# Mixer 0 of a hybrid decoder step: steps of joins, sample and group norms placed between the hops of a chunked scan

## The chip, the cores and the metric

The kernel runs on one core of a Trainium2 chip. The metric is device time in microseconds (us) of one execution; the median of three runs before the change is 1593.11 us (1591.4 to 1595.03). Engines are named as the profile names them: PE is TensorE's matrix multiplication and PEld its weight load, DVE is VectorE, ACT ScalarE, POOL GpSimd, and SP the engine that issues most of the DMAs.

## The reference

One inference step of a two-layer recurrent decoder for 512 prompt tokens and 8 samples of 4 tokens. Layer 0 mixes with two head groups beside each other: Hawk's RG-LRU (A) and RWKV-7 (B), with one input projection and one output projection. Layer 1 is HGRN2; each layer is followed by a SwiGLU feed-forward network. Everything is float32. Cut to the mixer that the change touches:

```python
def _rwkv_step(S, inp):
    r_t, w_t, k_t, v_t, kk_t, a_t = inp
    sk = jnp.einsum('bhvk,bhk->bhv', S, kk_t)
    S = (S * w_t[:, :, None, :] - sk[..., None] * (kk_t * a_t)[:, :, None, :]
         + v_t[..., None] * k_t[:, :, None, :])
    return S, jnp.einsum('bhvk,bhk->bhv', S, r_t)
...
for l in range(DEPTH):
    xn = rmsnorm(x, P['ln_mix'][l])
    if l % 2 == 0:
        p = xn @ P['w_in_ab'][j]
        u, conv_new = causal_conv(p[..., :W_A], conv_st[j], P['conv_w'][j], P['conv_b'][j])
        h, h_new = rg_lru(u, h_st[j], ...)
        out_a = jax.nn.gelu(p[..., W_A:P_A]) * h
        out_b, rS_new, shift_new = rwkv7(p[..., P_A:], shift_st[j], rS_st[j], ...)
        y = jnp.concatenate([out_a, out_b], axis=-1) @ P['w_out_ab'][j]
    ...
    x = x + y
    xf = rmsnorm(x, P['ln_ffn'][l])
    x = x + (silu(xf @ P['ffn_gate'][l]) * (xf @ P['ffn_up'][l])) @ P['ffn_down'][l]
```

In `rwkv7` the heads' output goes through a group norm per head, then a bonus term and a gate.

## The kernel before

Layer 0's mixer runs from the start to about 410 us, and only it is touched. A dense product is one 128x128 weight tile against 272 columns; float32 precision is kept by splitting weights into a high and a low half (`wh`, made by ACT at L210, and `wl = wf - wh`, made by DVE or POOL at L213), so each tile takes three products, wh twice and wl once.

RWKV-7 runs in chunks. For the 512 prompt tokens there are 8 chunks of 64. `scan()` (L881) works through them; each chunk c has three hops on PE with copies on DVE between them:

- hop A: S·W (last state S) is added to V·KB (the values V) in one half, `cr`, of a PSUM bank, and DVE copies it to `rhs` (L907); V·TM goes to the other half, `cs`;
- hop B: T·rhs, and DVE copies the result to `U` (L917);
- hop C: U·TM is added to `cs`, and DVE adds the decayed old state to it, the new `S` (L923); then V·KB of the next chunk and twelve groups of output products `ops`.

Between the hops `self.fill(18)` takes 18 dense products out of a list of other work: `rglru` (L1068), the input columns of group A, its convolution (`cf`, `uc`), gates (`gate`), recurrence (`v`, L1127) and GELU, and after it `lead` (L1148), the first blocks of the output projection (`acc<-cat`).

Beside the scan there are three more pieces, Python generators that advance by one step per `next`:

- `join(g)` (L771), four steps for each half of the chunks, which put together the triangular inverse `T` out of 32x32 blocks (`jps`);
- `sample()` (L986), the 8 samples: products `rpss`, `sps`, `opss`, a group norm, and for each pair of heads p an expansion `vx` on POOL, a product `dpss` on PE, an addition into the state `S0` on DVE (L1064) and its store `rS_s` on SP (L1065);
- `groupnorm(o)` (L942), whose first part (`g` in the plan) takes statistics in small operations on DVE and normalises `o` on POOL (L966), and whose second part (`h`) transposes on PE (`tps`), multiplies by the gate's weights (`gps`) and finishes on ACT and DVE (L979 to L984).

Two strings set the order. `MID` orders the features ahead of the scan ("a", "b", "r", "R" are steps of a head pair's features, "j" a join step, "x" values, "g" the output gate). `PLAN` orders the rest: "c" a chunk, "j" a join step, "s" a sample step, "f" a fill, "g" and "h" the parts of a group norm, "l" the start of `lead`, "d" the drain of the list. From "r3" in `MID` to the end of `PLAN`, `self.in_order` is "all": each PE instruction is chained to the one before it, so PE keeps the order of the code. After that only dense products are chained, and a scheduler places the rest. DVE, ACT, POOL and SP follow the scheduler throughout, each in one fixed order once built.

`lead` opens a pool `wo` for the weights of its second and third output column. That pool takes the room that `sample()` closes at its end.

Of the kernel before, what the change touches and what calls it, by code (L numbers as in the profile page):

```python
# [15 lines left out]
OP = mybir.AluOpType  # L16
# [7 lines left out]
NB = 8  # L24
NS = 4
NT = SEQ + NB * NS
# [7 lines left out]
NCH = SEQ // CH  # L34
# [16 lines left out]
AHEAD = 1  # L51
SQP = 6
VTB = 2
MID = 'v0 v2 v3 a3 v1 A3 b3 a1 r3 B3 A1 b1 a2 r0 R3 B1 A2 x b2 a0 x r1 x B2 A0 b0 R0 j x j r2 x j R1 j B0 g R2'
ENG = dict(d=1, kh=1, w0=1, w1=0, sg=1, tw=0, kf=2, km=1, kb=0, al0=1, al1=0, g1=0, g2=1, g3=0, oa=1, sp0=1, sp1=1)
LO = (3, 1)
FEAT = 'f0 b0 f2 f1 b1 b2 n0 f3 b3 n1'
PLAN = 'c1 j1 f12 j1 f8 c1 j1 f4 j1 s1 c1 s1 g0 c1 s3 h0 c1 s4 g1 c1 h1 s4 c1 s3 g2 l3 c1 c1 h2 f20 d0'
MSB = 3
HOP = (18, 18, 18)  # L60
KHB = 2
# [75 lines left out]
class Build:  # L137
# [205 lines left out]
    def mixer0(self):  # L343
# [4 lines left out]
        PTT = nc.gpsimd.tensor_tensor  # L348
# [390 lines left out]
        def receptance(p):  # L739
            rm = ph.tile([128, NT], F32, tag="pr", name="rm", bufs=RMB)  # L740
            proj(p, rm)
            E(f"w{p % 2}")(W[p][:, :, CH:], chunks(rm), chunks(eb[p][:, 1:]), OP.mult)
            for par in range(2):
                r = par_rows[par]
                PTT(Ws[par][p][r, CB:], rm[r, SEQ:], eb[p][r, 1 + SEQ:], OP.mult)
            pr = rm
            STT(pr, rm, v("rk", p), bon[p], op0=OP.mult, op1=OP.mult)
            yield
            scores(p)
            for h in range(2):  # L750
                c = slice(h * HF, (h + 1) * HF)
                ps = mps("bops")
                self.mm(ps[:, :HF], block64, pr[:, c])
                TT(bon[p][:, c], ps[:, :HF], vm[p][:, c], OP.mult)
# [129 lines left out]
        def first():  # L884
            return tc.high_priority(offset=CHAIN_PRIO)

        def scan():
            ops = S = None
            Vs = {}

            def inputs(c):
                heads(cr, lambda p: KB[p][:, 0, c], Vs[c], True, c == 0)

            with first():
                for c in range(nv - 1):
                    Vs[c] = load_v(c)
            yield
            for c in range(NCH):
                V = Vs[c]
                rhs = z.tile([128, 4, 64], F32, tag="rhs", name="rhs", bufs=2)  # L900
                U = z.tile([128, 4, 64], F32, tag="U", name="U", bufs=2)
                with first():
                    if c == 0:
                        inputs(0)
                    else:
                        heads(cr, lambda p: W[p][:, c, 0:CH], S, False, True)
                    nc.vector.tensor_copy(rhs, cr)  # L907
                    heads(cs, lambda p: TM[p][:, 0, c], V, True, False)
                    if c:
                        sp = z.tile([128, 4, 64], F32, tag="sp", name="sp")  # L910
                        PTT(sp, S, ebT[:, :, c:c + 1].to_broadcast([128, 4, 64]), OP.mult)
                self.fill(HOP[0])
                with first():
                    for p in range(4):
                        for r in par_rows:
                            self.mm(cr[r, p], T[r, c, p], rhs[r, p], start=False, stop=True, chain=True)
                    nc.vector.tensor_copy(U, cr)  # L917
                self.fill(HOP[1])
                with first():
                    heads(cs, lambda p: TM[p][:, 1, c], U, False, True)  # L920
                    Sn = z.tile([128, 4, 64], F32, tag="S", name="S", bufs=2)
                    if c:
                        TT(Sn, cs, sp, OP.add)  # L923
                    else:
                        nc.vector.tensor_copy(Sn, cs)
                    if c % 2 == 0:
                        ops = op.tile([128, 2, 4, 64], F32, tag="o", name="ops")
                    if c + 1 < NCH:
                        inputs(c + 1)
                    outputs(c, V, S, U, ops)  # L930
                    if c + nv - 1 < NCH:
                        Vs[c + nv - 1] = load_v(c + nv - 1)
                S = Sn
                if c % 2:
                    o = kp.tile([128, 8, 64], F32, tag="o", name="o", bufs=2)
                    ACT(o, ops.rearrange("p c q v -> p (c q) v"), AF.Copy)
                    obuf[c // 2] = o
                if c == NCH - 1:
                    nc.sync.dma_start(self.o["rS_p"], S)
                self.fill(HOP[2])  # L940
                yield
# [44 lines left out]
        def sample():  # L986
# [61 lines left out]
                ACT(o[:32, par::2], ops[q_rows[par]], AF.Copy)  # L1048
            yield
            yield from groupnorm(o, 32, 4)  # L1050
            for p in range(4):
                yield
                vx = sm.tile([128, NB, 64], F32, tag="vx", name="vx")
                for par in range(2):
                    sr = sc_rows[par]
                    PTT(vx[sr], zc[par][sr, p][:, None, :].to_broadcast([64, NB, 64]),
                        seqsel[sr][:, :, None].to_broadcast([64, NB, 64]), OP.mult)
                dp = self.ms.tile([128, NB, 64], F32, tag="m", name="dpss")
                for par in range(2):
                    sr = sc_rows[par]  # L1060
                    self.mm(dp[par_rows[par]], TMs[p][sr], vx[sr])
                sf = S0[:, p]
                PTT(sf, sf, ebT[:, p, NCH:][:, :, None].to_broadcast([128, NB, 64]), OP.mult)
                TT(sf, sf, dp, OP.add)  # L1064
                nc.sync.dma_start(self.o["rS_s"][:, p], sf)  # L1065
            self.close("sample")

        def rglru(i, before):  # L1068
# [100 lines left out]
        for e in PLAN.split():  # L1169
# [18 lines left out]
                next(halves[n])  # L1188
            else:
                next(halves[n], None)  # L1190
        self.in_order = self.last = None
        nc.sync.dma_start(self.o["shift_o"], shift_sb)
        nc.sync.dma_start(self.o["conv_o"], conv_sb)
        nc.sync.dma_start(self.o["h_o"], h_sb)
# [1 line left out]
        self.ms = self.open("ms", bufs=4, space=PSUM)  # L1196
        self.op = self.open("ops", space=PSUM)
        self.late_pools()
        for _ in groupnorm(obuf[3], 128, 3):
            pass  # L1200
        self.dump("oa0", oa[0], (128, NT))
        self.dump("ob0", bon[0], (128, NT))
        self.dump("ob3", bon[3], (128, NT))
        self.hilo(cat[7], oa[3])
        for j in range(4):
            self.hilo(cat[3 + j], bon[j], H1)
        self.lo_pool = 0
        return cat, ww0, ps0

    def late_pools(self):  # L1210
        self.np_ = self.open("norm")
# [9 lines left out]
        self.hilo_scaled(a, x, self.v(g, k))  # L1221
        return a

    def out_proj0(self, cat, ww, banks):
        nc = self.nc
        W = self.i["w_out_ab"]
        self.x = []
        xg = []
        self.norm_begin(self.sqp)
        H0, H1 = slice(0, SPLIT), slice(SPLIT, NT)  # L1230
        n = len(ww)
        pool = (self.open("wo2"), (2, 2 * (LEAD - n)))
        ww += [self.column(W[m], 0, KT, pool) for m in range(n, LEAD)]
        for m in range(KT):
            x = self.xp.tile([128, NT], F32, name=f"x{m}")
            nc.sync.dma_start(x, self.i["xT"][:, m, :])
            self.x.append(x)

        def run(m, ps, ks, c, first, last):
            for _ in self.products(ps, ww[m], cat, ks, c, first, last):  # L1240
                pass
            if last:
                x = self.x[m][:, c]
                nc.vector.tensor_tensor(x, ps[:, :c.stop - c.start], x, OP.add)

        def bank(i):
            if i % 7 < 3:
                return self.acc.tile([128, 512], F32, tag="acc", name="acc", bufs=3)
            return self.ms.tile([128, 512], F32, tag="m", name="acc")
        self.in_order = "chain"  # L1250
        for m in range(n):
            run(m, banks[m], (7,), H0, False, True)
        for m in range(n, LEAD):
            run(m, bank(m), range(KT), H0, True, True)
        banks = [bank(m + LEAD) for m in range(LEAD)]
        for m in range(LEAD):
            run(m, banks[m], (0, 1, 2, 7), H1, True, False)
        for m in range(LEAD):
            run(m, banks[m], (3, 4, 5, 6), H1, False, True)
            xg.append(self.finish_x(self.x[m], m, "ln_ffn0", self.act_b))  # L1260
        self.in_order = self.last = None
        self.wide = True
        for m in range(LEAD, KT):
            def ev(ps, h, c):
                nc.vector.tensor_tensor(self.x[m][:, c], ps, self.x[m][:, c], OP.add)
            self.dense(W[m], cat, ev)
            xg.append(self.finish_x(self.x[m], m, "ln_ffn0", self.act_b))
        self.close("wo2", "wo", "keep")
        return xg
# [501 lines left out]
```

## Time and profile before

| what | value |
| --- | --- |
| median of 3 runs | 1593.11 us |
| the profiled execution | 1591.88 us |
| its span in the trace | 1590.1 us |
| around the span | 1.8 us |
| PE busy | 1495.7 us, 94% |
| DVE, ACT, POOL busy | 832.9, 547.7, 402.0 us |
| HBM read and written | 120.13 and 10.50 MB, 82 GB/s |
| mean granted clock of PE | 0.963 of full |

The profile is of one execution. Its page gives the busy time of each engine, then the span in 40 slices of about 40 us, where a digit is the busy share in tenths and `PEclk` the clock that PE was granted, in tenths of full speed. A list of instructions gives start and duration in microseconds, engine, line, operation, result and operands (numbers of buffers left out), shape, and in brackets the idle time before it with what ended that. "x16" is a run of sixteen. In the trace a small float32 product counts twice as many PE instructions as in the program.

### The profile page before, as it was taken

How to read it: one execution, taken by the hardware profiler on the slowest of the kernel's cores; microseconds unless marked ns; L12 is line 12 of the kernel's file. 1: busy time of each engine (PE TensorE's matmuls, PEld its weight loads, DVE VectorE, ACT ScalarE, POOL GpSimd, SP SyncE). 2: the span in 40 equal slices, each digit the busy share in tenths (PEclk: the TensorE clock that was granted, in tenths of full speed). 3: DMA queues.
4: the chain of work that ended last, by engine and by line, in shares of the span. 5: the costliest groups of instructions: out<-in, count | busy, mean ns of one | idle time of the engine just before them, and what ended most of it. 6: DMA issues, size and time to landing. Idle time of an engine off the chain costs nothing.

```text
span 1590.1 us, 34915 instructions
## 1 busy us (share of the span) xinstructions
PE 1495.7 (94%) x14688; PEld 1441.9 (91%) x14688; DVE 832.9 (52%) x1542; ACT 547.7 (34%) x982; POOL 402.0 (25%) x520
## 2 busy tenths in 40 slices
PE   7988888675999999999999999999999999999998
PEld 6877777555999999999999999999999999999997
DVE  7775344355454434443467657666675443444344
ACT  5642144134333223322344333333443322233234
POOL 4572243331211001100123344444441110110010
PEclk9997999777999999999999999999999999999999
DMA  4122221013022322322223222222333223222321
GB/s 161 61 69 83 57 77 35 24 58 104 30 91 85 90 88 85 94 87 87 91 82 113 69 98 92 79 89 95 103 118 97 85 87 91 90 93 82 93 74 57
DMA packets 87405, 132.88 MB, mean 84 GB/s; under 512 B 24369, under 2 KB 30385, under 8 KB 87121
## 3 DMA queue, kind: packets, MB, share of 16 engines
q1 hardware_dynamic: 87248, 130.66, 26.4%
q8 instruction: 115, 1.88, 0.5%
q14 instruction: 42, 0.34, 0.1%
HBM read 120.13 MB, written 10.50 MB: 82 GB/s over the span
## 4 chain that ended last, share of the span: by engine, by line
PE 78%; DVE 2%; ACT 1%; DMA 1%; POOL 1%; issue 0%; DVEq 0%; POOLq 0%; ACTq 0%; SPq 0%
PE acc L179 70%; PE lv L179 2%; PE ops L179 1%; PE ch L179 1%; DMA wf<-w_out_ab 1%; PE dpss L179 0%; PE ds L179 0%; PE tr L1586 0%; PE gps L179 0%; PE nps L179 0%; PE opsm L179 0%; PE d L179 0%; PE opsq L179 0%; DMA x<-xT 0%; PE gate L179 0%
## 5 line engine op out<-in xcount | busy, mean ns | idle before, releaser
L179 PE MATMUL acc<-xg,wh 128*128 128x272 f32 x4544 | 884.1, 293 | 11.6 <-ACT xg L270 6.4
L179 PEld LDWEIGHTS acc<-xg,wh 128*128 128x128 f32 x4544 | 721.3, 191 | 20.4 <-ACT xg L270 6.4
L179 PE MATMUL acc<-xg,wl 128*128 128x272 f32 x2272 | 652.1, 292 | 0.0
L210 ACT ACTIVATE wh<-wf 128x512 fp32r<-128x512 f32 (+1 forms) x404 | 250.8, 621 | 683.7 <-PE acc L179 546.1
L179 PEld LDWEIGHTS acc<-xg,wl 128*128 128x128 f32 x2272 | 429.8, 191 | 3.1 <-issue 0.8
L213 DVE TENSOR_TENSOR wl<-wf,wh 128x512 fp32r<-128x512 f32 (+1 forms) x373 | 267.5, 718 | 194.8 <-ACT wh L210 169.6
L1290 POOL TENSOR_TENSOR S<-S,rstd 128x272 f32<-128x272 f32 x88 | 74.6, 848 | 645.2 <-ACT S L1289 645.2
L179 PE MATMUL acc<-h,wh 128*128 128x272 f32 x1280 | 236.9, 288 | 0.0
L179 PEld LDWEIGHTS acc<-h,wh 128*128 128x128 f32 x1280 | 198.0, 188 | 0.0
L179 PE MATMUL acc<-h,wl 128*128 128x272 f32 x640 | 176.7, 287 | 0.0
L179 PEld LDWEIGHTS acc<-h,wl 128*128 128x128 f32 x640 | 118.1, 188 | 0.0
L1293 DVE TENSOR_TENSOR hh<-acc,S 128x272 f32<-128x272 f32 x88 | 38.8, 441 | 126.3 <-PE acc L179 124.7
L179 PE MATMUL acc<-cat,wh 128*128 128x272 f32 (+2 forms) x512 | 97.3, 290 | 0.0
L179 PEld LDWEIGHTS acc<-cat,wh 128*128 128x128 f32 x512 | 80.5, 189 | 0.2
L1289 ACT ACTIVATE S<-t 128x272 f32<-128x272 f32 x88 | 37.8, 431 | 122.5 <-DVE t L1288 122.5
L1310 DVE TENSOR_TENSOR x<-acc,x 128x272 f32<-128x272 f32 x80 | 35.0, 438 | 81.7 <-PE acc L179 81.4
L1288 DVE TENSOR_TENSOR t<-acc,rstd 128x272 f32<-128x272 f32 x88 | 38.7, 441 | 70.5 <-PE acc L179 70.4
L179 PE MATMUL acc<-cat,wl 128*128 128x272 f32 (+2 forms) x256 | 72.7, 290 | 0.0
L288 POOL TENSOR_TENSOR ssq<-ssq,sq 128x544 f32<-128x544 f32 x33 | 46.5, 1409 | 91.2 <-ACT sq L287 90.7
L213 POOL TENSOR_TENSOR wl<-wf,wh 128x512 fp32r<-128x512 f32 x31 | 41.6, 1347 | 86.8 <-ACT wh L210 86.8
L1560 POOL TENSOR_TENSOR K<-K,G 128x256 f32<-128x256 f32 (+1 forms) x48 | 39.1, 815 | 78.6 <-PE lv L179 78.6
L179 PEld LDWEIGHTS acc<-cat,wl 128*128 128x128 f32 x256 | 47.9, 189 | 0.2
(367 smaller groups left out, 1574.0 us busy)
## 6 DMA issues: line engine op xcount, KB each, us to landing
wf<-gate SPq DMA_DIRECT2D x88, 256.0 KB
wf<-up SPq DMA_DIRECT2D x88, 256.0 KB
wf<-down SPq DMA_DIRECT2D x72, 256.0 KB
wf<-w_in_c SPq DMA_DIRECT2D x64, 256.0 KB
wf<-w_in_ab SPq DMA_DIRECT2D x44, 256.0 KB
x<-xT SPq DMA_DIRECT2D x16, 272.0 KB
wf<-w_out_ab SPq DMA_DIRECT2D x16, 256.0 KB
S<-hS SPq DMA_DIRECT2D x8, 512.0 KB
```

The lines of the kernel that those rows point to most:

```text
L179: return self.seq(self.nc.tensor.matmul(out, lhsT, rhs, start=start, stop=stop, skip_group_check=True), chain)
L210: nc.scalar.activation(wh[:, :n], wf[:, :n], AF.Copy)
L213: eng.tensor_tensor(wl[:, :n], wf[:, :n], wh[:, :n].bitcast(F32), OP.subtract)
L288: eng.tensor_tensor(self.ssq, self.ssq, t, OP.add)
L1288: nc.vector.tensor_tensor(t[:, c], ps, rs()[:, c], OP.mult)
L1289: nc.scalar.activation(S[:, c], t[:, c], AF.Silu)
L1290: nc.gpsimd.tensor_tensor(S[:, c], S[:, c], rs()[:, c], OP.mult)
L1293: nc.vector.tensor_tensor(hh[:, c], ps, S[:, c], OP.mult)
L1310: nc.vector.tensor_tensor(x[:, c], ps, x[:, c], OP.add)
L1560: PTT(kv[:, :, 0], kv[:, :, 0], g2[:, :, 1, None].to_broadcast([128, m, b]), OP.mult)
```

## The change

- `scan()` yields after each of the three hops, so that a chunk takes three steps of the plan. `PLAN` puts one step of the sample, a join or a group norm behind nearly every hop. All four steps of the second join run within the first chunks, and `lead` starts after the last sample step.
- V·KB of a chunk moves from the preceding chunk's hop C to its own hop A, ahead of S·W. V·TM moves from hop A to hop B, ahead of T·rhs.
- In `receptance` a yield stands ahead of the bonus products, and `MID` has a second "R" entry per head pair.
- In the sample, `expand(p)` makes `vx` and decays the state for head pair p one step ahead of its `dpss`.
- The last group norm is split: its first part is the last but one entry of `PLAN`; `rest()` runs its second part, and splits the second half of `cat`, ahead of the third column (m == 2) of the output projection's second half. PE keeps the written order up to there.

```diff
-PLAN = 'c1 j1 f12 j1 f8 c1 j1 f4 j1 s1 c1 s1 g0 c1 s3 h0 c1 s4 g1 c1 h1 s4 c1 s3 g2 l3 c1 c1 h2 f20 d0'
+PLAN = 'c1 f8 c1 j1 c1 j1 c1 j1 c1 j1 c1 s1 c1 g0 s1 c1 s1 c1 s1 c1 h0 s1 c1 s1 c1 s1 c1 g1 s1 c1 s1 c1 s1 c1 h1 s1 c1 s1 c1 s1 c1 g2 s1 c1 s1 c1 s1 c1 h2 s1 l3 c1 c1 c1 g3 d0'
...
             scores(p)
+            yield
             for h in range(2):
...
                 with first():
-                    if c == 0:
-                        inputs(0)
-                    else:
+                    inputs(c)
+                    if c:
                         heads(cr, lambda p: W[p][:, c, 0:CH], S, False, True)
                     nc.vector.tensor_copy(rhs, cr)
-                    heads(cs, lambda p: TM[p][:, 0, c], V, True, False)
...
                 self.fill(HOP[0])
+                yield
                 with first():
+                    heads(cs, lambda p: TM[p][:, 0, c], V, True, False)
                     for p in range(4):
...
                 self.fill(HOP[1])
+                yield
                 with first():
...
-                    if c + 1 < NCH:
-                        inputs(c + 1)
                     outputs(c, V, S, U, ops)
...
-            for p in range(4):
-                yield
+            def expand(p):
                 vx = sm.tile([128, NB, 64], F32, tag="vx", name="vx")
...
+                sf = S0[:, p]
+                PTT(sf, sf, ebT[:, p, NCH:][:, :, None].to_broadcast([128, NB, 64]), OP.mult)
+                return vx
+
+            yield
+            vx = expand(0)
+            for p in range(4):
+                yield
                 dp = self.ms.tile([128, NB, 64], F32, tag="m", name="dpss")
...
                 sf = S0[:, p]
-                PTT(sf, sf, ebT[:, p, NCH:][:, :, None].to_broadcast([128, NB, 64]), OP.mult)
                 TT(sf, sf, dp, OP.add)
                 nc.sync.dma_start(self.o["rS_s"][:, p], sf)
+                if p < 3:
+                    vx = expand(p + 1)
...
-        self.in_order = self.last = None
...
-        for _ in groupnorm(obuf[3], 128, 3):
-            pass
...
         self.hilo(cat[7], oa[3])
-        for j in range(4):
-            self.hilo(cat[3 + j], bon[j], H1)
         self.lo_pool = 0
-        return cat, ww0, ps0
+
+        def rest():
+            for _ in halves[3]:
+                pass
+            for j in range(4):
+                self.hilo(cat[3 + j], bon[j], H1)
+        return cat, ww0, ps0, rest
...
-        self.in_order = "chain"
...
         for m in range(LEAD):
+            if m == 2:
+                rest()
             run(m, banks[m], (0, 1, 2, 7), H1, True, False)
```

How the rows stand on three engines follows; lines are those of the program they come from. First PE in the third chunk (c = 2), from the end of hop C's state product on. Before:

```order
L179 MATMUL ch<-U,TM_1013 64x64 x2
L179 MATMUL ch<-V,KB_247 64x64 x2
L179 MATMUL ch<-V,KB_248 64x64 x2
L179 MATMUL ch<-V,KB_249 64x64 x2
L179 MATMUL ch<-V,KB_250 64x64 x2
L179 MATMUL ops<-V,SV_1006 64x64 x2
L179 MATMUL ops<-S,W_243 64x64 x2
```

With the change, the same chunk's hop C ends with these rows; its twelve groups of `ops` and 18 dense products stand ahead of them:

```order
L179 MATMUL acc<-xg,wh 128x272 x2
L179 MATMUL tps<-ident,o 64x64 x16
L179 MATMUL gps<-sg,g_241 128x128 x4
L179 MATMUL rpss<-S_3106,am_3110 32x64 x16
L179 MATMUL rpss<-Zs_3116,Ws_254 32x64
L179 MATMUL rpss<-Zs_3117,Ws_258 32x64
L179 MATMUL ch<-V,KB_247 64x64 x2
L179 MATMUL ch<-V,KB_248 64x64 x2
L179 MATMUL ch<-V,KB_249 64x64 x2
L179 MATMUL ch<-V,KB_250 64x64 x2
L179 MATMUL ch<-S,W_243 64x64 x2
```

V·KB stood directly behind U·TM; now the output products, a fill, the second part of a group norm and a sample step stand between, and S·W follows V·KB.

Second, DVE in the same chunk, from the copy `U` to the state `S`. Before:

```order
L1127 SCALAR_TENSOR_TENSOR v_267<-a,tr 128x544
L917 COPY U<-ch 128x256
L1093 SCALAR_TENSOR_TENSOR cf<-UX,vec,cf 128x568 x2
L1095 SCALAR_TENSOR_TENSOR uc<-UX,vec,cf 128x512
L1097 SCALAR_TENSOR_TENSOR uc<-UX,vec,cf 128x32
L1101 TENSOR_TENSOR gg<-acc,rstd 128x272
L923 TENSOR_TENSOR S<-ch,sp 128x256
```

With the change:

```order
L1126 SCALAR_TENSOR_TENSOR ti<-ti,uc 128x544
L918 COPY U<-ch 128x256
L1128 SCALAR_TENSOR_TENSOR uc<-uc,tr 128x544
L1134 MEMSET a 128x8
L1084 TENSOR_TENSOR UX<-acc,rstd 128x240
L1086 TENSOR_TENSOR UX<-acc,rstd 128x8x4
L1130 SCALAR_TENSOR_TENSOR tr<-uc,ti 128x544
L1133 TENSOR_TENSOR tr<-tr,t_3331 128x8
L1135 SCALAR_TENSOR_TENSOR v_267<-a,tr 128x544
L1101 SCALAR_TENSOR_TENSOR cf<-UX,vec,cf 128x568
L925 TENSOR_TENSOR S<-ch,sp 128x256
```

The scan `v` stood ahead of `U` and now stands behind it, with the gate's products, between `U` and `S`.

Third, SP's queue at the end of the mixer. `rS_s` are the sample's state stores; before, `wf_4473` and `wf_4479` are `lead`'s first output column and the next four (4485 to 4503) its second and third, in the pool `wo`. Before:

```order
L209 DMA wf_4479<-w_out_ab 128x512
L209 DMA wf_5022<-w_out_ab 128x512
L1193 DMA conv_o<-conv_sb_2526 128x108
L1065 DMA rS_s<-S0_3039 128x512 x3
L209 DMA wf_4485<-w_out_ab 128x512
L209 DMA wf_4491<-w_out_ab 128x512
L209 DMA wf_4497<-w_out_ab 128x512
L209 DMA wf_4503<-w_out_ab 128x512
```

With the change the second and third column are 4526 to 4544:

```order
L209 DMA wf_5022<-w_out_ab 128x512
L1071 DMA rS_s<-S0_3106 128x512 x2
L209 DMA wf_5028<-w_out_ab 128x512
L209 DMA wf_5092<-w_out_ab 128x512
L1071 DMA rS_s<-S0_3106 128x512
L209 DMA wf_4526<-w_out_ab 128x512
L209 DMA wf_4532<-w_out_ab 128x512
L209 DMA wf_4538<-w_out_ab 128x512
L209 DMA wf_4544<-w_out_ab 128x512
```

The stores no longer stand together: two weight loads come between, and the last store, of the last sample step, is directly ahead of the second column's loads.

More of the change, by code (lines that the diff above doesn't have):

```diff
@@ L53 @@
 VTB = 2
-MID = 'v0 v2 v3 a3 v1 A3 b3 a1 r3 B3 A1 b1 a2 r0 R3 B1 A2 x b2 a0 x r1 x B2 A0 b0 R0 j x j r2 x j R1 j B0 g R2'
+MID = 'v0 v2 v3 a3 v1 A3 b3 a1 r3 B3 A1 b1 a2 r0 R3 B1 A2 x R3 b2 a0 x r1 x B2 A0 b0 R0 j x R0 j r2 x R1 j B0 R1 j g R2 R2'
 ENG = dict(d=1, kh=1, w0=1, w1=0, sg=1, tw=0, kf=2, km=1, kb=0, al0=1, al1=0, g1=0, g2=1, g3=0, oa=1, sp0=1, sp1=1)
@@ L1198, in mixer0 @@
         self.late_pools()
-        for _ in groupnorm(obuf[3], 128, 3):
-            pass
-        self.dump("oa0", oa[0], (128, NT))
-        self.dump("ob0", bon[0], (128, NT))
-        self.dump("ob3", bon[3], (128, NT))
         self.hilo(cat[7], oa[3])
-        for j in range(4):
-            self.hilo(cat[3 + j], bon[j], H1)
         self.lo_pool = 0
-        return cat, ww0, ps0
+        def rest():
[4 more added lines that the diff above has]
+        return cat, ww0, ps0, rest
     def late_pools(self):
@@ L1222, in finish_x, with out_proj0 @@
         return a
-    def out_proj0(self, cat, ww, banks):
+    def out_proj0(self, cat, ww, banks, rest):
         nc = self.nc
```

## The prediction

> **What bounds the kernel now.** The page comes first: which engine sets the end, and in which of the 40 slices it does not work.
>
> ```profile
> PE 1495.7 (94%) x14688; PEld 1441.9 (91%) x14688; DVE 832.9 (52%) x1542; ACT 547.7 (34%) x982; POOL 402.0 (25%) x520
> PE   7988888675999999999999999999999999999998
> PEclk9997999777999999999999999999999999999999
> ```
>
> TensorE (PE) is busy for 94% of the span and full from the eleventh slice on. The holes are in slices 5 to 10 of 40 us each, with a low granted clock beside them. That is mixer 0, all that the change touches. Its windows come next (window, length, busy us of PE, PEld, DVE, ACT, POOL with counts, granted clock, DMA share, GB/s).
>
> ```profile
> 181.00:402.00 221.00, 161.17 (x2550) 140.66 (x2551) 96.62 (x210) 75.29 (x126) 67.27 (x89) 0.81 0.19 59
> 180.00:190.00 10.00, 6.73 (x270) 6.02 (x270) 2.93 (x7) 1.25 (x2) 1.38 (x6) 0.72 0.52 128
> 190.00:200.00 10.00, 9.47 (x219) 8.63 (x219) 2.25 (x6) 1.58 (x4) 1.27 (x1) 0.94 0.01 3
> 300.00:310.00 10.00, 2.58 (x45) 2.15 (x43) 5.43 (x18) 2.22 (x7) 2.44 (x3) 0.70 0.00 0
> 340.00:350.00 10.00, 7.71 (x46) 4.04 (x46) 5.92 (x17) 0.00 (x0) 3.14 (x3) 0.50 0.20 79
> 390.00:400.00 10.00, 2.07 (x33) 1.96 (x34) 5.42 (x19) 1.94 (x4) 1.04 (x1) 0.50 0.36 138
> 410.00:420.00 10.00, 10.00 (x77) 10.00 (x77) 2.52 (x5) 2.77 (x5) 0.00 (x0) 1.00 0.10 28
> ```
>
> From 181 to 402 us PE works 161.17 of 221.00: **59.8 us idle**. No other engine is full (DVE 97, ACT 75, POOL 67), so chains from engine to engine set the time. The clock averages 0.81; if it is either 0.5 or 1, it was at half for 0.19 × 2 × 221 = 84 us. What PE stood for, from 140 to 410 us (total, times, longest):
>
> ```profile
> PE ch L179 <- DVE rhs L907: 14.4, 8, 5.2
> PE tps L179 <- POOL o L966: 11.7, 1, 11.7
> PE ch L179 <- DVE S L923: 11.3, 6, 6.6
> PE dpss L179 <- POOL vx L1056: 7.5, 2, 6.3
> PE tps L973 <- POOL o L966: 7.4, 1, 7.4
> PE jps L179 <- issue: 3.7, 3, 2.1
> PE jps L179 <- DVE SV L531: 1.7, 1, 1.7
> ```
>
> `ch` is the scan's chain, `tps` a group norm's transposition, `dpss` the sample's state product, `jps` a small product of the features and joins. The third chunk shows how such a wait arises (start, duration, what ran, idle time before it):
>
> ```profile
> 225.68 0.68 PE L179 MATMUL ch<-S,W 64*64 64x64 f32 x16
> 229.76 1.12 PE L179 MATMUL ch<-V,TM 64*64 64x64 f32 x16 [3.40 <-DVE rhs L907]
> ...
> 232.34 0.66 PE L179 MATMUL acc<-xg,wh 128*128 128x272 f32 x2
> ...
> 233.02 0.66 PE L179 MATMUL acc<-xg,wh 128*128 128x272 f32 x2
> ...
> 238.46 0.68 PE L179 MATMUL ch<-U,TM 64*64 64x64 f32 x16
> 241.50 0.68 PE L179 MATMUL ch<-V,KB 64*64 64x64 f32 x16 [2.36 <-DVE S L923]
> ```
>
> V·TM stands right behind S·W and waits for `rhs`, the copy of that product; V·KB stands right behind U·TM and waits for `S`. PE keeps the written order, so everything behind waits too. After the pause three dense products take 0.68 us (232.34 to 233.02), 0.227 each; at full clock 77 take 10.00 us, 0.130 each. Work at half clock thus loses 0.43 of its time. With PE busy for some two thirds of the 84 us (a little under its 73% of the whole stretch; the windows at 0.50 show 77% and 21%), 55 us, the **loss is about 24 us**, and the work itself 161 − 24 = 137 us.
>
> **The change part by part.** *Value products and steps between hops.* V·TM now stands a hop of 18 dense products (2.3 us) behind S·W, and V·KB behind the output products, 18 dense ones and a step. Whether DVE delivers within that, these rows price: a queue of DVE, a table load of ACT, and PE's output products, `tps` and `gps`.
>
> ```profile
> 234.56 2.42 DVE L1127 TENSOR_TENSOR_SCAN v<-a,tr 128x544 f32<-128x544 f32 x1
> 236.90 0.39 DVE L917 COPY U<-ch 128x256 f32<-128x256 f32 x1
> 237.21 2.60 DVE L1093 SCALAR_TENSOR_TENSOR cf<-UX,vec,cf 128x568 f32<-128x568 f32 x2
> ...
> 241.03 0.41 DVE L923 TENSOR_TENSOR S<-ch,sp 128x256 f32<-128x256 f32 x1
> 331.67 1.29 DVE L1127 TENSOR_TENSOR_SCAN v<-a,tr 128x544 f32<-128x544 f32 x1
> 224.71 1.28 ACT L1116 ACT_TABLE_LOAD   x1
> 327.01 0.28 PE L179 MATMUL ops<-V,SV 64*64 64x64 f32 x4
> 328.50 0.52 PE L179 MATMUL acc<-xg,wh 128*128 128x272 f32 x2
> 382.94 1.15 PE L179 MATMUL tps<-ident,o 64*64 64x64 f32 x32
> 384.02 1.16 PE L179 MATMUL gps<-sg,g 128*128 128x128 f32 x8
> ```
>
> Third chunk: between `U` and `S` DVE now has the gate's and the convolution's operations, at the 1.3 us of an undisturbed scan and about 0.7 for each of four wide ones some 4.7 us, 7 if they stretch as at 234.56 and 237.21. PE has 18 dense products ahead of U·TM (2.3), then output products (327.01 to 328.50, 1.5), 18 dense (2.3), tps and gps (2.3): 8.4 us. I take no wait; up to 4 us if the square root on ACT, behind two table loads, comes late. Fifth chunk: `U` stands behind that square root, 0.5 us, at most 3. With the joins the first two chunks keep the issue pause of 2.1, and DVE's copies of T ahead of `S` cost 1.1: 3.2.
>
> Where DVE's scan took 1.29 us alone and 2.42 beside two POOL operations, I add 6 us over the chunks for such stretches; with 1.29 throughout the forecast would be 6 us lower. [...]
>
> *Sample and group norms as steps.* Prices: a small norm operation, `o` on POOL, `dpss`.
>
> ```profile
> 280.10 0.17 DVE L965 SCALAR_TENSOR_TENSOR st<-st 128x8 f32<-128x8 f32 x1
> 345.35 1.04 POOL L966 TENSOR_TENSOR o<-o,st 128x512 f32<-128x512 f32 x1 [1.27 <-DVE st L965]
> 345.04 1.06 PE L179 MATMUL dpss<-vx,TMs 64*64 64x512 f32 x1
> ```
>
> Sixth chunk: the sample's `tps` comes one hop (2.4 us) behind S·W. DVE then still has `rhs` 0.4, two operations of the last norm 1.1, a reduction 0.7 and 12 small ones at 0.2, then POOL's `o` 1.0: 5.6, a wait of 3.3 (0 to 5). Seventh chunk: the third `vx` on POOL stands behind a copy that needs the scan's result, 1.6; the norm's last operation on DVE is behind two splits of `cat`, 1.4: 3.0 (0 to 6). The waits for `vx` (7.5) and `o` (7.4) of before go in exchange. The last norm's `tps` now comes after the second half's first products, and its 11.7 us are covered.
>
> *The output weights.* `lead`'s second and third weight blocks lie in room that the sample frees: their loads wait until its last state store has landed. That store was at 346.8 and the blocks were wanted 20 us later; now the last sample step stands right ahead of the last chunk, and the blocks are wanted within it.
>
> ```profile
> 346.13 0.69 DVE L1064 TENSOR_TENSOR S<-S,dpss 128x512 f32<-128x512 f32 x1 [0.95 <-PE dpss L179]
> 349.40 0.82 SPq L209 DMA_DIRECT2D wf<-w_out_ab  x2
> 352.42 1.15 ACT L210 ACTIVATE wh<-wf 128x512 fp32r<-128x512 f32 x2 [15.36 <-DMA wf<-w_out_ab]
> 353.12 3.01 POOL L213 TENSOR_TENSOR wl<-wf,wh 128x512 fp32r<-128x512 f32 x2 [6.74 <-ACT wh L210]
> ```
>
> From the state's addition to `wh` 6.3 us passed, and a `wh` takes 0.6. With some 1.5 us of queue on DVE ahead, `wh` is there 8.4 us after the last dpss. PE has V·KB, S·W, two gate pairs and nine dense products, 2.5 us: a stall of 5.9. The next `wh` is behind a table load and the square root, 1.2; its `wl` on POOL (1.3 to 1.5) behind a copy that waits for the scan and a wide product, 4.5: 11.6 with what is left over. The blocks after these reach the output projection 4.4 us late (0 to 8). Together **16 us, against 11.7 us there before**; this part loses.
>
> *Features.* The R split puts a yield before products that waited 1.7; the transfers of the triangular solve bound that place as well, so I take 1 us (0 to 1.7). The value transfers of the first chunks arrive as PE asks for them (0 to 0.7, in the rest).
>
> *Sum.* Idle: 3.2 + 0 + 0.5 + 3.3 + 3.0 + 11.6 + 4.4 + 1 for the other hops + 6 for stretches = 33, so 59.8 − 33 = **27 us less**. Clock: the half-clock stretch of the first join lasted 0.28 × 2 × 10 + 0.06 × 2 × 10 = 6.8 us and costs 6.8 × 0.43 = 2.9 where PE is busy. Pauses remain at the join and in the sixth and seventh chunk (8.8), and about 4 us at the weights: 13 against 24, **11 less**. With the features 39: the profiled run, 1591.9 (span 1590.1), becomes 1553, and as the median of the runs, 1593.1, lies 1.2 above it, **1554 us**.
>
> A row against pauses as the only cause: at 180:190 the clock fell to 0.72 although the longest join pause was 2.1. [...]
>
> **Rivals.** *Nearly no wait is left*: DVE and ACT are under half busy, and if queues meet as undisturbed rows say and weights land early, 12 us of idle and 6 of clock stay: 48 + 18 + 1 = 67, 1526 to 1540. Against: the weights' chain is one of transfers. *Stretched queues*: the third, fifth and seventh chunk pay their upper ends (4 + 2.5 + 3) and two to three more clock falls (8): 1554 + 18 = 1572, 1567 to 1585. For: the doubled rows at 234.56 and 237.21. *Short pauses don't touch the clock*: 8.8 less, 1545. *The waits only change place*: each weight block pays the 6.3 us chain and the sample's norm its whole queue: 55 us idle, clock as before, 1586 to 1598. *Slower*: pauses recur in every hop, at least every 6.8 us, and the clock stays at half from the third chunk to the last, as in 340:350. Some 100 of the 137 us of work lie there and would lose 100 × 0.43 / 0.57 = 75 instead of 24, against 27 won: 24 slower, 1617. It decides from about 67 us of work at half clock (51 us lost). That the change does not do what it says is excluded by the orders shown above.
>
> **How the numbers follow.** Forecast (1540 to 1567) 0.55, no wait left 0.11, stretched 0.15, short pauses 0.04, changed place 0.07, slower 0.08. The range 1535 to 1586 takes in the forecast, the clock rival, the stretched one and half of the first: 0.8. A measurement of this kernel tells some 0.2% from no change. Faster beyond that: 0.55 + 0.11 + 0.15 + 0.04 and 0.01 of the changed places, 0.86; within 0.05; slower 0.08 + 0.01 = 0.09.
>
> **What would show it.** Waits for `rhs` and `S` together under 5 us instead of 27; PE idle from 181 us to the end of the mixer about 33; the longest waits of PE on `wh` and `wl` of the output weights, with ACT waiting for their transfers right behind the last state store; half clock for some 45 us instead of 84. Wrong if `rhs` and `S` still cost 10 us, if the clock stays at half across whole chunks, or if the first output products never wait for weights.

## The result and the profile after

| | before | with the change |
| --- | --- | --- |
| median of runs | 1594.07 us (4 runs, 1591.4 to 1595.43) | 1543.36 us (4 runs, 1542.56 to 1546.71) |
| profiled execution, its span | 1591.88, 1590.1 us | 1542.56, 1540.8 us |

The four runs before are the three named at the start and one more. The ratio is 0.9688, with a 95% interval of 0.9668 to 0.9708: 51 us less. The page of the changed kernel, PE's busy time and its slices:

```profile
PE 1480.7 (96%) x14688; PEld 1432.2 (93%) x14688; DVE 831.7 (54%) x1542; ACT 549.4 (36%) x983; POOL 401.9 (26%) x520
PE   7988899879999999999999999999999999999998
PEclk9999999879999999999999999999999999999999
```

The same 14688 instructions are busy 15 us less, and of the holes two slices remain. The windows cut the changed run so that the rest after the stretch is as long as before (window, length, busy time of PE, PEld, DVE, ACT, POOL, granted clock, DMA share, GB/s):

```profile
181.00:352.00 171.00, 145.65 (x2528) 130.78 (x2526) 94.10 (x206) 73.94 (x122) 67.58 (x88) 0.91 0.24 76
352.00:1540.00 1188.00, 1180.11 (x10076) 1159.39 (x10076) 618.11 (x1093) 398.58 (x728) 244.10 (x283) 1.00 0.28 87
```

For the kernel before, the same question has this answer:

```profile
402.00:1590.00 1188.00, 1180.36 (x10060) 1160.33 (x10059) 616.65 (x1092) 395.83 (x722) 244.09 (x283) 1.00 0.28 87
```

In these windows of 1188 us, PE is busy for 1180 in both kernels. So nearly all of the difference lies between 181 us and the end of the mixer: 221 us have become 171. PE's idle time there fell from 59.8 to 25.4 us, 34.5 less. The clock's mean rose from 0.81 to 0.91, which is 0.09 × 2 × 171 = 31 us at half clock instead of 84. What PE still waited for, from 140 to 400 us:

```profile
PE acc L179 <- ACT wh L210: 7.3, 2, 4.4
PE tps L973 <- POOL o L966: 4.0, 1, 4.0
PE acc L179 <- POOL wl L213: 3.1, 2, 2.2
PE dpss L179 <- POOL vx L1055: 2.6, 2, 2.1
...
PE ch L179 <- issue: 1.9, 2, 1.5
...
PE ch L179 <- DMA V<-vT: 1.5, 1, 1.5
PE ch L179 <- DVE U L918: 1.5, 2, 0.9
...
PE ch L179 <- DVE rhs L907: 0.3, 1, 0.3
```

The waits for `rhs` and `S`, 14.4 and 12.6 us before (11.3 at L923, as shown with the prediction, and 1.3 at L925), are 0.3 and nothing. In the third chunk the chain now looks like this on PE and on DVE:

```profile
222.73 0.68 PE L179 MATMUL ch<-V,TM 64*64 64x64 f32 x16
...
227.51 0.68 PE L179 MATMUL ch<-U,TM 64*64 64x64 f32 x16
...
235.38 0.68 PE L179 MATMUL ch<-V,KB 64*64 64x64 f32 x16
```

```profile
224.65 0.41 DVE L918 COPY U<-ch 128x256 f32<-128x256 f32 x1
...
228.18 1.13 DVE L1133 TENSOR_TENSOR tr<-tr,t 128x8 f32<-128x8 f32 x1
229.34 1.29 DVE L1135 TENSOR_TENSOR_SCAN v<-a,tr 128x544 f32<-128x544 f32 x1
230.54 0.79 DVE L1101 SCALAR_TENSOR_TENSOR cf<-UX,vec,cf 128x568 f32<-128x568 f32 x1
231.25 0.42 DVE L925 TENSOR_TENSOR S<-ch,sp 128x256 f32<-128x256 f32 x1
```

`S` is ready at 231.67 us, 3.5 us after U·TM. V·KB comes at 235.38 and has no wait in its row. DVE is no faster than before, and an operation on 8 columns took 1.13 us here, while POOL made a `wl` (from 227.98 to 229.27 us). It is only that nothing on PE stands there waiting for it.

### The profile page after: what moved, and what is told of

Same layout as the page of the kernel before. It is cut to its first block, busy times and chain, and to the rows that moved or that the text cites. A ratio compares the mean times of both kernels' runs of the same rounds, so it can differ in the third digit from the quotient of the medians.

```text
span 1540.8 us, 34923 instructions
## 1 busy us (share of the span) xinstructions
PE 1480.7 (96%) x14688; PEld 1432.2 (93%) x14688; DVE 831.7 (54%) x1542; ACT 549.4 (36%) x983; POOL 401.9 (26%) x520
## 4 chain that ended last, share of the span: by engine, by line
PE 85%; DVE 6%; ACT 3%; DMA 2%; issue 2%; POOL 1%; SPq 1%; DVEq 0%; ACTq 0%; POOLq 0%
PE acc L179 74%; PE lv L179 2%; PE ops L179 2%; PE ch L179 1%; PE jps L179 1%; SPq L698 1%; DMA wf<-w_out_ab 1%; PE ds L179 0%; PE tr L1593 0%; PE nps L179 0%; DVE Y L685 0%; DVE wl L213 0%; ACT wh L210 0%; DMA wd<-down 0%; PE opsm L179 0%
## 5 line engine op out<-in xcount | busy, mean ns | idle before, releaser
L179 PE MATMUL acc<-xg,wh 128*128 128x272 f32 x4544 | 877.2, 291 | 12.6 <-ACT xg L270 6.2
```

The source lines that it names most:

```text
L179: return self.seq(self.nc.tensor.matmul(out, lhsT, rhs, start=start, stop=stop, skip_group_check=True), chain)
```

## The experiments

Each kernel was measured against the kernel before on the same chip; the ratio is to that.

**The value products put back.** Steps stay between the hops; V·TM and V·KB return to their old places.

```diff
-                    inputs(c)
-                    if c:
+                    if c == 0:
+                        inputs(0)
+                    else:
                         heads(cr, lambda p: W[p][:, c, 0:CH], S, False, True)
                     nc.vector.tensor_copy(rhs, cr)
+                    heads(cs, lambda p: TM[p][:, 0, c], V, True, False)
...
+                    if c + 1 < NCH:
+                        inputs(c + 1)
                     outputs(c, V, S, U, ops)
```

> The changed kernel with V.TM put back right behind S.W and V.KB right behind U.TM; steps stay between the hops. Theory (the gain needs the distance between a chain product and the product that waits for its copy): V.TM waits for rhs again, 8 times at least 0.5 us, V.KB for S, 0.6 us in the chunks with an empty DVE queue and 1.5, 3 and 5 in the third, fifth and seventh, 17 us together, and 3 to 6 of clock: 1560 to 1568. Rival (the steps between the hops bring it, wherever the value products stand): within 6 us of the changed kernel, below 1550.

Measured: 1566.02 us, ratio 0.9827 (0.981 to 0.9843), 23 us above the changed kernel, as the theory said. Its waits:

```profile
PE ch L179 <- DVE rhs L908: 12.4, 8, 3.4
PE ch L179 <- DVE S L926: 11.1, 6, 3.6
...
PE tps L976 <- POOL o L969: 3.2, 1, 3.2
```

The waits for `rhs` and `S` are back, nearly at their old sums. But those of the bunched steps, 7.5 for `vx`, 7.4 and 11.7 for `o`, are 3.2 in all. So the other edits together are worth 28 us without this one. By the rival it would have been 44 or more; the theory's range, 1560 to 1568, has it. They cure other waits.

**The value products alone, in the kernel before.** The same lines the other way round, and nothing else.

> The kernel before with the two value products moved and nothing else. Theory: the waits for rhs (14.4) and S (12.6) mostly go, the bunched steps' waits for vx (7.5), o (7.4) and the last group norm (11.7) stay; 18 to 25 us of idle and some 6 of clock less: 1562 to 1572. Rival (steps bring it): the waits move to T.rhs, U.TM and the bunched steps, less than 10 us won: over 1584.

Measured: 1563.58 us, ratio 0.981 (0.9795 to 0.9824), 30 us less than before. Its waits:

```profile
PE tps L179 <- POOL o L963: 11.8, 1, 11.8
PE tps L970 <- POOL o L963: 7.4, 1, 7.4
PE ch L179 <- DVE U L916: 5.4, 2, 4.5
PE dpss L179 <- POOL vx L1053: 4.8, 3, 2.6
...
PE ch L179 <- DVE rhs L906: 0.2, 1, 0.2
```

This is the other half of the picture: `rhs` is gone, the bunched steps remain, and `U` has become a wait. Two halves of 30 and 28 us add to 58 where 51 were measured together, so they overlap by only some 7 us.

**The last group norm back to the scheduler.** `g3` leaves the plan, the chaining of all of PE's work ends with the plan, and the norm runs as a whole behind it.

```diff
-... c1 c1 c1 g3 d0'
+... c1 c1 c1 d0'
...
+        self.in_order = self.last = None
...
+        for _ in groupnorm(obuf[3], 128, 3):
+            pass
         self.hilo(cat[7], oa[3])
+        for j in range(4):
+            self.hilo(cat[3 + j], bon[j], H1)
...
```

> The changed kernel with the last group norm placed by the scheduler again behind the plan. Theory (its fixed place is worth most of the 11.7 us wait of before): PE waits 6 to 11 us for o in the output projection, 1549 to 1555. Rival (PE stands there for weights anyway): within 3 us of the changed kernel.

Measured: 1546.59 us, ratio 0.9699 (0.9684 to 0.9713). That is 3.2 us above the changed kernel, with intervals that overlap: between the two expectations, nearer the rival. The trace has a wait of 6.3 us for `o`, which the theory wanted, but the 3.0 us wait for weights beside it is gone: PE stood there for the one instead of the other, and 3.3 us longer.

```profile
PE tps L179 <- POOL o L966: 6.3, 1, 6.3
PE acc L179 <- ACT wh L210: 4.1, 1, 4.1
```

**The sample two hops sooner.** Two plan entries become "s2" (first hop of the third chunk, second of the sixth), and the last two "s1" go.

> The changed kernel with two sample steps in the first hop of the third chunk and two in the second of the sixth, so that the sample and its last store end two hops sooner. Theory (the 10 us of waits for output weights hang on the last store): the weights come some 6 us sooner, 4.4 and 2.2 us waits shrink to under 2, half clock after 327 us goes: 1532 to 1539. Rival (the chain of transfers or ACT's and POOL's queues hold the weights back by themselves): within 3 us of the changed kernel.

Measured: 1541.58 us, ratio 0.9672 (0.9653 to 0.9691), 1.8 us less, within the noise. By the total the rival was right, by the trace the theory: the waits for `wh` fell from 7.3 to 3.0, the longest from 4.4 to 2.2, and those for `wl` on POOL are gone. But PE waits longer for the `o` of the sample's norm, which was brought forward, and for `U`, which DVE makes. `o` and `U` rose from 4.0 and 1.5:

```profile
PE tps L973 <- POOL o L966: 7.2, 1, 7.2
PE ch L179 <- DVE U L918: 5.2, 2, 4.0
...
PE acc L179 <- ACT wh L210: 3.0, 2, 2.2
```

**The sample's norm step one hop later.**

```diff
-... c1 h1 s1 c1 s1 c1 s1 c1 g2 ...
+... c1 h1 s1 c1 c1 s2 c1 g2 ...
```

> The changed kernel with the step that transposes the sample's normalised output one hop later (none in the first hop of the sixth chunk, two in the second). Theory (the 4.0 us wait there is the norm's queue of small operations on DVE against one hop of cover, and the half clock behind it, 10.3 us, follows from the wait): the wait falls under 1.5 us, the half clock goes, 3 + 3 us: 1536 to 1540. Rival (the queue is late as a whole, the wait moves to U or to vx): within 2 us of 1543.

Measured: 1538.7 us, ratio 0.9652 (0.9632 to 0.9671). That is 4.7 us below the changed kernel, within the expected 1536 to 1540; the two intervals just touch (0.9671 and 0.9668). The wait for `o` in the sample's norm no longer stands among PE's waits; the others that are shown above stay within 0.6 of theirs, and only the pauses in the chain for which the profile shows no cause are longer, 3.6 against 1.9. The 4.0 of wait went, as the theory said. But half clock did not become less: the mean granted clock is 0.981 of full in either profiled execution, which is some 58 us at half clock over spans of 1535.6 and 1540.8. So the profiles show the gain as wait, and the 3 us of clock that the theory added were not won.

**And the first output column's products together.**

```diff
             for m in range(n):
                 ps0.append(self.acc.tile([128, 512], F32, tag="acc", name="acc", bufs=3))
                 yield from self.products(ps0[m], ww0[m], cat, (0, 1, 2), H0, first=True)
-            for m in range(n):
                 yield from self.products(ps0[m], ww0[m], cat, (3, 4, 5, 6), H0)
```

> The same, and the first output column takes all its 21 products before the second column's first, instead of 9. Theory (weights come 6 us behind the last store whatever stands ahead, so that 12 products of cover are 1.6 us off the 4.4 us wait, and the half clock behind it shortens): 2 to 5 us below the kernel with the later step alone, 1532 to 1537. Rival (the later waits for wl and the scan take it back): no difference to it.

Measured: 1532.37 us, ratio 0.9615 (0.9597 to 0.9632); once more, beside the last experiment:

> The kernel with the later norm step and the first column's products together once more, beside the one above on the same chip: 1530 to 1535 by either.

1530.92 us, ratio 0.9609 (0.9591 to 0.9627). That is 6.3 and 7.8 us below the kernel with the later step alone, where 2 to 5 were expected; the interval of the first touches that kernel's, the second's doesn't. In the first of the two runs the waits for the weights are these:

```profile
PE acc L179 <- ACT wh L210: 5.0, 2, 3.4
...
PE acc L179 <- POOL wl L213: 0.9, 1, 0.9
```

The wait of 4.4 us has become 5.0 − 3.4 = 1.6 (the 3.4 is that of a later block), and those for `wl` fell from 3.1 to 0.9.

**vx in the step of its product.** `expand` is undone, with an empty step ahead so that the products keep their places.

```diff
...
-            vx = expand(0)
             for p in range(4):
                 yield
+                vx = sm.tile([128, NB, 64], F32, tag="vx", name="vx")
...
-                if p < 3:
-                    vx = expand(p + 1)
...
```

> The changed kernel with vx made on POOL in the same step as its product dpss, the products at the same places. Theory (the step ahead hides two POOL operations, 2.2 us, behind a hop): three to four waits of 2 us come in front of dpss, one less where POOL was late anyway, and 1 to 3 of clock: 1549 to 1554. Rival (POOL has caught up by the time PE arrives): within 2 us of 1543.

Measured: 1544.56 us, ratio 0.9687 (0.9666 to 0.9707), no difference. The wait for `vx` is 2.6 us, as with the edit. Over the mixer, POOL's instructions stand in the same order in both traces, but for one decay of the state (246.00 us in the changed kernel) and one small copy, which change places. Every `vx` keeps its place: the scheduler puts it there whichever way the code is written.

**The features as before.** The old `MID`, and no yield ahead of the bonus products.

> The changed kernel with the features as before (no yield ahead of the bonus products, the old order of the entries). Theory (1.7 us of wait were won, part of it bounded by the transfers of the triangular solve): 1 to 3 us above the changed kernel, 1544 to 1547. Rival (the transfers bound it alone): within 1 us.

Measured: 1546.03 us, ratio 0.9693 (0.9672 to 0.9715). The medians are 2.7 us apart, as expected, but the intervals overlap, so the gain is not shown by the times; the trace has the old wait again.

```profile
PE jps L179 <- DVE SV L531: 1.5, 1, 1.5
```

**The second half's first products ahead of columns 4 and 5**, on the kernel with the two steps above.

```diff
         for m in range(n):
             run(m, banks[m], (7,), H0, False, True)
-        for m in range(n, LEAD):
-            run(m, bank(m), range(KT), H0, True, True)
-        banks = [bank(m + LEAD) for m in range(LEAD)]
-        for m in range(LEAD):
-            if m == 2:
-                rest()
-            run(m, banks[m], (0, 1, 2, 7), H1, True, False)
...
+        banks = [wide(), wide(), acc()]
+        for m in range(n):
+            run(m, banks[m], (0, 1, 2, 7), H1, True, False)
+        rest()
+        for m in range(n, LEAD):
+            run(m, acc(), range(KT), H0, True, True)
...
```

The lines left out make the two kinds of banks, and give columns 4 and 5 the whole of their second half at the end, in one go; `rest()` moves ahead of them, too.

> The kernel with the later norm step and the first column's products together; in the output projection the second half's first products of columns 1 to 3, whose weights are there, now come ahead of columns 4 and 5. Theory (the 3.4 us wait there is a transfer and a split that start when the scan's room is free, and 36 dense products, 4.7 us, cover it; the half clock at 334 us goes with it): 3 to 6 us below 1532, 1526 to 1530. Rival (the last group norm's o, wanted sooner now, takes its place): no difference, 1530 to 1535.

Measured: **1525.66 us**, ratio 0.9583 (0.956 to 0.9607), the lowest of all, 5.3 us below the same kernel without it on the same chip. The intervals overlap a little (up to 0.9607 here, from 0.9591 there). Its window and two of its waits:

```profile
181.00:336.00 155.00, 141.94 (x2536) 127.44 (x2536) 93.58 (x202) 72.94 (x120) 65.34 (x88) 0.94 0.26 82
...
PE acc L179 <- ACT wh L210: 1.6, 1, 1.6
...
PE tps L179 <- POOL o L966: 1.1, 1, 1.1
```

Of 155 us PE is idle for 13.1. The 3.4 us wait for a later block is gone, as the theory said, and of the rival's wait for `o` 1.1 us came.

## Why the prediction was right, and which terms were mis-sized

It named 1554 us in a range of 1535 to 1586, and 1543.36 was measured. The way the gain splits was right, too: most of it idle time, the rest nearly all the clock. Three of its signs came: 0.3 us for `rhs` and `S` together, the longest wait for `wh` behind the last store, and less half clock, though 31 us and not some 45. By its own steps:

- *Value products and steps.* "I take no wait" in the third chunk: right, `S` had 3.7 us to spare. The fifth chunk was to wait 0.5 for `U`, and 0.9 was measured. For the first two chunks 3.2 were set down for an issue pause and the joins' copies; the trace has 1.9 of issue and 1.5 for the transfer of the first values, which had been given 0 to 0.7. The size held, but one of its causes did not, so that it fits is in part luck.
- *Stretches.* 6 us were added for DVE operations that take longer beside POOL's. Such rows are there: `tr` on 8 columns took 1.13 us in the rows above, while POOL made a `wl`, and 0.17 at 330.47 us, where POOL stood idle. (Of the two rows that the prediction calls doubled, the one at 237.21 holds two operations.) But in the third chunk they fell within the cover of a hop, and the waits for `U` that are left come to 1.5 us in all. This term was nearly all too much. The sentence beside it, by which undisturbed durations would give 6 us less, was the nearer one, though not because the stretches were absent.
- *Sample and norms.* 3.3 for the sample's `tps`, 4.0 measured; 3.0 in the seventh chunk, against 2.6 for `vx` and, by the rows of the rest, 1.2 for `ti` and 1.0 for `tr`, both results of a gate on ACT.
- *The output weights.* 16 us (11.6 and 4.4) were expected; measured are 7.3 for `wh` (4.4 and, in the output projection, 3.0), 3.1 for `wl` and 0.6 at a gate, for DVE's addition to the state, 11.0. The chain to the first `wh` was as described:

```profile
319.96 0.68 DVE L1070 TENSOR_TENSOR S<-S,dpss 128x512 f32<-128x512 f32 x1
320.67 0.34 SPq L1071 DMA_DIRECT2D rS_s<-S  x1
323.36 6.45 SPq L209 DMA_DIRECT2D wf<-w_out_ab  x4
326.19 0.63 ACT L210 ACTIVATE wh<-wf 128x512 fp32r<-128x512 f32 x1 [0.67 <-DMA wf<-w_out_ab]
326.87 0.52 PE L179 MATMUL acc<-cat,wh 128*128 128x256 f32 x2 [4.39 <-ACT wh L210]
```

  From the state's addition to `wh` 6.2 us passed, where 6.3 was taken from before. The stall behind it is 4.4 and not 5.9, because the addition on DVE came 0.9 us behind the end of the last dpss and not 1.5, and PE had somewhat more to do. What follows it was over-priced, 0.9 and 2.2 instead of 5.7, because the order in the queues was another: ACT made the second `wh` at 327.08 us, ahead of the table load and the square root (329.02), and POOL its `wl` directly behind the first. The copy and the wide product, for which POOL waits on the scan, came only then (332.04 and 332.31), and so it was the third `wl` that PE waited 2.2 us for. That the wait depends on the last store is supported by the sample that ends sooner, where the waits for `wh` come to 3.0 instead of 7.3.
- *Clock.* 13 us of loss were to remain of 24. The half-clock stretches behind the first one, at 184 us and shown below, are these windows:

```profile
276.20:286.50 10.30, 8.63 (x62) 8.15 (x62) 1.44 (x6) 1.67 (x5) 3.26 (x3) 0.51 0.04 12
306.90:310.30 3.40, 3.40 (x64) 3.39 (x64) 3.37 (x7) 0.00 (x0) 2.03 (x2) 0.52 0.02 5
327.40:341.10 13.70, 10.66 (x111) 9.80 (x113) 4.01 (x6) 4.17 (x6) 6.53 (x6) 0.51 0.15 50
```

  With the 3.4 of the first, PE was busy for 26 of the 31 us, which by the same 0.43 is an estimated 11 lost. So 13 us were won and not 11.
- *Features.* 1 us expected; undoing the edit cost 2.7 by the medians, which is not clear of noise, and brought back a wait of 1.5 for `SV`. The counts of PE's instructions show little of it: the stretch has 22 fewer (2528 against 2550), but only 7 of them ran ahead of 181 us (2087 against 2080). The others differ because the windows end at other work: 40 small ones of the last group norm now stand behind 352 us, and 22 more dense ones of the output projection ahead of it.

Sum: 34.5 us of idle time and 15.5 of PE's busy time (161.17 less 145.65) make the 50 by which the stretch is shorter. The forecast had 27, and 11 of clock and 1. The clock's 13 are an estimate with 0.43; the 2.5 that are left of the 15.5 no run divides further. The term that was off most is the idle sum, 33 expected and 25.4 measured, by the allowance for stretches (6) and by the weights (5). Together these are more than the 7.6 us that it missed, because the smaller waits were somewhat longer than set down.

The rivals: "the waits only change place" fell by the waits above. The stretched queues and the clock that never recovers did not come. "Short pauses don't touch the clock" named 1545, nearer to 1543.36 than the forecast, but for a reason that the trace refutes: half clock stood behind the 1.5 us pause for the first values and behind the waits of the seventh chunk, none of them over 2.2 us. "Nearly no wait is left" was not this change, but it is what the last experiment reaches, at 1525.66 just under the 1526 to 1540 that the rival gave.

One thing the working did not see is that `expand` has no effect. It let the waits for `vx` go without asking which edit does it; 2.6 us of them stayed, and POOL makes every `vx` at the same place with `expand` and without it.

## What to carry to other kernels

Where one engine keeps a written order and another copies its results, what counts is how much work stands between a product and the first one that needs its copy: moving two groups of products that were ready anyway won 30 us without making any operation faster, and the other edits together, most of which break up bunches of dependent steps, won 28 without it. What each of these is worth alone was not measured, but for the last norm, the features and `expand`. When steps are spread out, look at what each one releases: the last store of the sample held the room for the output weights, and bringing all its steps forward only moved the wait to the norm and to `U`, while one step later and better cover for the weights won 18 us more. An edit in generated code is not an edit in an engine's queue: compare the orders before pricing it.

## What was not expected of the hardware

In the traces of the kernel before and the changed one, every stretch between two changes of the granted clock is 3.41 us long or a whole multiple of it (3.4 to 17.1 us at half clock). The half-clock stretches of the changed kernel between 181 and 352 us last one, three, one and four such spans (3.4, 10.2, 3.4 and 13.7 us), not the 6.8 us by which the prediction priced each. Windows cut at these spans show it (the first number behind the length is PE's busy time, the third from the end the clock):

```profile
180.48:183.89 3.41, 1.91 (x25) 1.64 (x24) 1.49 (x6) 0.66 (x1) 0.75 (x2) 1.00 0.67 164
183.89:187.30 3.41, 3.41 (x17) 3.41 (x16) 0.31 (x1) 0.00 (x0) 0.35 (x2) 0.50 0.58 178
187.30:190.72 3.42, 3.30 (x263) 3.02 (x263) 0.84 (x2) 0.28 (x1) 0.00 (x0) 1.00 0.02 7
...
272.64:276.05 3.41, 1.22 (x9) 0.92 (x7) 3.10 (x11) 2.93 (x5) 1.27 (x1) 1.00 0.11 35
276.05:279.47 3.42, 1.60 (x9) 1.53 (x10) 0.55 (x4) 0.93 (x4) 1.85 (x2) 0.50 0.12 43
279.47:282.88 3.41, 3.41 (x40) 3.23 (x40) 1.00 (x3) 0.26 (x1) 1.40 (x2) 0.50 0.03 5
282.88:286.29 3.41, 3.41 (x15) 3.18 (x15) 0.00 (x0) 0.49 (x1) 0.00 (x0) 0.50 0.00 0
286.29:289.71 3.42, 3.42 (x74) 2.99 (x74) 0.87 (x2) 2.15 (x3) 0.62 (x1) 1.00 0.00 0
...
299.95:303.36 3.41, 1.60 (x13) 1.38 (x11) 3.41 (x6) 1.21 (x2) 2.12 (x3) 1.00 0.31 93
303.36:306.77 3.41, 2.14 (x4) 0.38 (x4) 3.41 (x4) 0.00 (x0) 3.26 (x4) 1.00 0.20 77
306.77:310.19 3.42, 3.34 (x62) 3.34 (x64) 3.39 (x7) 0.00 (x0) 2.16 (x2) 0.50 0.02 5
```

A span in which PE worked 1.91 of 3.41 us is followed by one at half clock, and that one, full of work, by full clock again. A span at half clock with 1.60 of work is followed by another, and behind the full one at 279.47 came one more. So the pause of 1.5 us for the first values, in the span that ends at 183.89, had one span at half clock behind it, and the prediction's price of 6.8 us for every pause came from one case.

PE's work in a span does not by itself tell what follows. At 299.95 the clock stayed behind 1.60 us of work, and at 303.36 it fell behind 2.14. In the two traces, of the spans at full clock between 30 and 420 us, 20 were followed by half clock, with PE busy for up to 0.64 of the span, and 164 were not, with PE busy for as little as 0.47. What decides between these two the runs leave open.
